# Low-rank decay, learning rate and latent queries from stacked float32r parts instead of float32 matmuls

## The chip, the cores and the metric

The kernel runs on one core of a Trainium2 chip. The metric is the device time of one execution in microseconds (us). Three runs of the kernel before took 1474.29, 1471.72 and 1472.41 us; the median is 1472.41 us. The engines are named as in the profile: PE is TensorE, PEld its weight loads, DVE is VectorE, ACT is ScalarE, POOL is GpSimd, and SP issues DMAs.

## The reference, cut to what matters

Two layers run over 1152 tokens (1024 of a prompt and 8 samples of 16). Each layer projects the normalised input once, and four branches take their columns from it. The change touches two of them: branch A takes two low-rank products of 64 ranks each, and branch B takes its queries from 192 ranks.

```
# branch A: wd and ad are 64 columns each of the shifted projection
w_log = -softplus(-(rw_w0 + tanh(wd) @ rw_w2)) - 0.5
decay = exp(-exp(w_log))
a = sigmoid(rw_a0 + ad @ rw_a2)
kk = normalised(k * rw_kk);  k = k * (1 + (a - 1) * rw_ka)
# per token: s = s * decay + (s @ -kk) (kk * a)^T + v k^T;  y = s @ r
...
# branch B: 192 ranks, 4 heads of 64 + 32 columns
qa = rms_norm(zb[..., :192], mla_qa_g)
q = (qa @ mla_w_uq).reshape(b, t, 4, 96)
q_nope = rms_norm(q[..., :64], ...);  q_rope = rope(rms_norm(q[..., 64:], ...), pos)
# then block-causal attention over keys made from 128 latent ranks
```

Everything is float32.

## The kernel before, in words

Features lie on the 128 partitions and tokens on the columns, in three groups (g = 0, 1, 2) of 384 tokens. Most products go through PE as float32r in three passes: an operand is split in two parts, hi (a float32r copy) and lo (the difference), and hi·hi, hi·lo and lo·hi are summed in PSUM. `project` streams 24 tiles of 128 features per layer in this way (tiles `xh`, `xl`, `wh`, `wl`; 24 matmuls of 384 columns for a tile and group), and small work runs between its matmuls in generators that are advanced by ticks. The order on each engine is that of the program after a scheduler of the tile framework has moved instructions; tiles are rotated through pools of fixed size (`ea` 8, `m` 8, `xl` 3, PSUM `st` 2, `pj` 2, `b` 4).

Stage A opens a layer. The first feature tile WDAD holds the 64 decay ranks on partitions 0 to 63 and the 64 learning-rate ranks on 64 to 127. `shift_sink` mixes each group with its neighbouring token (DVE, L377 to L387) into the tile `z6`, and `tanh_part` (L401 to L405) puts the decay ranks through tanh. `a_elem(i, g, k)` runs six times in a layer, for two halves i of the features and three groups g: `pw` (PSUM `st`) and `pa` (PSUM `b`) are plain float32 matmuls of 64 rows of `wlo` with 64 rows of `z6` (L429 to L432), `pk` is the square sum; then come about a dozen operations on DVE and ACT, among them the running sum (L441) and four products of 64 partitions into `kb` (L471, L477). When all of `kb` and `ar` of a group are there, `systems` builds the chunks' triangular systems with PE, masks them on DVE (`ns`, L504, two buffers) and writes them to DRAM (`nd`). `solve` reads `nd` back, inverts one system per partition in a long alternation of two DVE instructions (L528, L530), and writes the inverses (`dd`, issued by ACT, L542, L543); the recurrence over the chunks starts from these.

Branch B's queries (`query`, L1190 to L1205) come behind the last projection tile. For a head h and a group g, `ps` (PSUM `st`) sums a float32 matmul over ranks 0 to 127 (`qx`, weights behind the keys in `Kt`, an `m` tile) and one over the last 64 ranks (weights `wq1`, which lie in `cx`). ACT squares it (L1196), DVE multiplies it into the tile X (L1198), `split(q, (V, V))` makes hi and lo of the squares on DVE (a cast, L91, and a subtraction, L92), two matmuls sum them over partitions (`b<-sp,cr`), ACT makes the inverse root in two steps (L206, L207), and DVE multiplies (L1205). Eight such units (groups 0 and 1) run in a loop with two ahead, and beside each a `value(j)` (one float32 matmul of 256 columns, one ACT copy, L1211). The four units of group 2 (256 columns) run in a generator beside the prompt attention, which follows. The output projection closes the layer.

Of the kernel before, what the change touches and what calls it, by code (L numbers as in the profile page):

```python
# [10 lines left out]
F32 = mybir.dt.float32  # L11
F32R = mybir.dt.float32r
# [6 lines left out]
D = 1024  # L19
# [11 lines left out]
# projection tiles, in the order in which they are streamed  # L31
# [6 lines left out]
# columns of the per-feature vectors  # L38
# [4 lines left out]
# constant matrices  # L43
# [5 lines left out]
def tile_trunk(ctx: ExitStack, tc: tile.TileContext, *aps):  # L49
# [34 lines left out]
    def split(src, by, view=lambda t: t):  # L84
        """two exact parts of a tile; by: engines of the copy and of the difference"""
# [9 lines left out]
    def total(out, m, parts, start=True, stop=True):  # L95
        """sums over partitions of a tile in two parts, weighted by small integers"""
        mm(out, m, parts[0], start, False)
        mm(out, m, parts[1], False, stop)
# [16 lines left out]
    # Work that runs beside the large products: lanes of generators, each advanced by one step per tick.  # L115
# [37 lines left out]
    # running input of the layer: 4 tiles of [128, 2, G] per token group, and sums of squares  # L153
# [15 lines left out]
    # sums over partitions: of all, of each half; of the halves of queries  # L169
# [21 lines left out]
    def raw_weights(fi, src):  # L191
        """a whole tile of weights ahead of its splitting"""
# [16 lines left out]
    def recip1p(t):  # L209
        """t <- 1 / (1 + t)"""  # L210
# [11 lines left out]
    def load_weights(n):  # L222
        """weights as two exact parts, in pairs of k-tiles in their order of use"""
# [14 lines left out]
    def project(keys, hi, lo, sinks, ticks=(3,)):  # L238
        """one tile of features, or several of them side by side, group after group of tokens"""
# [58 lines left out]
    # zero at the first token of each chunk (64 tokens; 16 in the last 128 columns)  # L298
# [11 lines left out]
    # rows of the chunks' inverses, zero off the diagonal blocks  # L310
    # (half chunks of 64 rows; the room behind each lets the diagonal blocks lie at equal distances)
# [3 lines left out]
    def whole(t, c, cols):  # L315
        """the two halves of chunk c"""
        return t[2 * c:2 * c + 2, 0:128 * cols].rearrange("x (s t) -> x s t", s=64)

    def diagonal(t, i, n, cols, first=0):
        """the n x n blocks of the halves' matrices: block b of rows at columns first + b n"""  # L320
# [14 lines left out]
    for l in range(L):  # L335
        last_layer = l == L - 1
# [968 lines left out]
        for u in units[:2]:  # L1305
            next(u)
# [246 lines left out]
```

## Time and profile before

| | us | share |
|---|---|---|
| median of three runs | 1472.41 | |
| span of the profiled execution (the only time of its own that the page gives) | 1470.1 | |
| PE busy | 1395.4 | 95% |
| DVE busy | 782.2 | 53% |
| ACT busy | 751.9 | 51% |
| POOL busy | 436.8 | 30% |
| TensorE clock, mean granted share | | 0.988 |

The median lies 2.3 us above the span. Busy shares are averages over stages. A float32 matmul stands in the trace as two records ("x2"), a float32r matmul as one. Records of back-to-back matmuls overlap, so that the price of one is read from start to start. The idle time of an engine is put down to the instruction that it then waited for.

### The profile page before, as it was taken

The page shows a single profiled execution, that of the slowest core. Times are in us where ns is not written, and L with a number is a line of the kernel's source. Part 1 is how long each engine was busy: PE and PEld are TensorE (multiplying, and loading weights), DVE is VectorE, ACT ScalarE, POOL GpSimd, SP SyncE. Part 2 cuts the span into 40 slices and gives each one's busy share as a digit, 9 for nine tenths or more (in the row PEclk, how much of TensorE's full clock was granted, in tenths as well). Part 3 has the DMA queues.
Part 4 walks back from the last instruction along what each step waited for, and adds up shares of the span by engine and source line. Part 5 has one row for each costly group of instructions (what it writes and reads, how often), then busy time and mean ns, then how long its engine had stood idle before and what let it go on. Part 6 is the DMA issues. An engine that isn't in the chain of part 4 may idle for free. (4 is left out here: it accounts for less than half of the span.)

```text
span 1470.1 us, 26810 instructions
## 1 busy us (share of the span) xinstructions
PE 1395.4 (95%) x9938; PEld 1158.6 (79%) x9938; DVE 782.2 (53%) x1762; ACT 751.9 (51%) x2017; POOL 436.8 (30%) x575
## 2 busy tenths in 40 slices
PE   4898899999999999999979988999999999999999
PEld 3678778888987776689967787888899778666998
DVE  7985944445136457742387857433632464677211
ACT  6672244655366667642257522455644666666210
POOL 4514314346321110322262333332652111112320
PEclk9999999999999999999989999999999999999999
DMA  7113241111212114033300123221021111131232
GB/s 224 48 33 81 52 101 49 55 46 38 93 42 70 53 31 130 6 114 97 87 22 29 52 66 73 77 69 47 30 78 60 57 53 55 37 109 43 69 96 77
DMA packets 116594, 97.38 MB, mean 66 GB/s; under 512 B 46128, under 2 KB 111344, under 8 KB 116464
## 3 DMA queue, kind: packets, MB, share of 16 engines
q1 hardware_dynamic: 76776, 73.74, 17.1%
q10 hardware_dynamic: 39688, 21.94, 5.0%
q8 instruction: 78, 1.28, 0.4%
q14 instruction: 52, 0.43, 0.1%
HBM read 71.48 MB, written 24.16 MB: 65 GB/s over the span
## 5 line engine op out<-in xcount | busy, mean ns | idle before, releaser
L76 PE MATMUL pj<-xh,wh 128*128 128x384 f32 x1152 | 413.6, 360 | 18.5 <-ACT xh L273 7.3
L76 PE MATMUL pj<-xl,wh 128*128 128x384 f32 x1152 | 395.4, 343 | 4.1 <-POOL xl L275 3.1
L76 PE MATMUL pj<-xh,wl 128*128 128x384 f32 x1152 | 394.8, 343 | 0.0
L235 POOL TENSOR_TENSOR wl<-wr,wh 128x256 fp32r<-128x256 f32 x200 | 155.0, 783 | 484.3 <-ACT wh L234 421.9
L76 PEld LDWEIGHTS pj<-xh,wh 128*128 128x128 f32 x1152 | 220.2, 191 | 45.2 <-ACT sho L390 11.5
L76 PEld LDWEIGHTS pj<-xl,wh 128*128 128x128 f32 x1152 | 220.3, 191 | 11.8 <-POOL xl L275 5.5
L76 PEld LDWEIGHTS pj<-xh,wl 128*128 128x128 f32 x1152 | 220.0, 191 | 7.6 <-issue 6.4
L76 PE MATMUL pj<-yh,wh 128*128 128x384 f32 x384 | 130.0, 339 | 2.4 <-DVE x L1376 2.4
L76 PE MATMUL pj<-yh,wl 128*128 128x384 f32 x384 | 129.2, 336 | 0.0
L76 PE MATMUL pj<-yl,wh 128*128 128x384 f32 x384 | 129.0, 336 | 0.0
L234 ACT ACTIVATE wh<-wr 128x256 fp32r<-128x256 f32 x200 | 80.8, 414 | 93.9 <-PE pj L76 45.9
L76 PEld LDWEIGHTS pj<-yh,wh 128*128 128x128 f32 x384 | 72.5, 189 | 3.7 <-DVE x L1376 2.8
L235 POOL TENSOR_TENSOR wl<-m,wh 128x256 fp32r<-128x256 f32 x56 | 43.5, 787 | 102.2 <-ACT wh L234 75.8
L76 PEld LDWEIGHTS pj<-yh,wl 128*128 128x128 f32 x384 | 72.7, 189 | 0.1
L76 PEld LDWEIGHTS pj<-yl,wh 128*128 128x128 f32 x384 | 72.6, 189 | 0.1
L1251 ACT ACTIVATE X<-b,ng 128x512 f32<-128x512 f32 (+3 forms) x96 | 54.9, 575 | 28.8 <-DVE ng L1243 24.7
L76 PEld LDWEIGHTS st<-X,X 128*64 128x64 f32 x576 | 35.7, 136 | 31.7 <-DVE mx L1239 6.3
L76 PE MATMUL b<-sp,cr 128*128 128x384 f32 (+3 forms) x192 | 58.7, 386 | 1.0 <-POOL sp L92 0.6
L1239 DVE TENSOR_REDUCE mx<-b 128x1 f32<-128x512 f32 (+3 forms) x96 | 53.0, 552 | 8.3 <-PE b L76 6.9
L1372 DVE TENSOR_TENSOR pt<-pj,pt 128x384 f32<-128x384 f32 x24 | 13.4, 557 | 80.6 <-PE pj L76 80.6
L234 ACT ACTIVATE wh<-m 128x256 fp32r<-128x256 f32 x56 | 22.5, 413 | 62.0 <-PE pj L76 60.9
L76 PE MATMUL st<-X,X 128*64 128x128 f32 x576 | 53.6, 283 | 0.3
(295 smaller groups left out, 2556.9 us busy)
## 6 DMA issues: line engine op xcount, KB each, us to landing
wr<-in_win_dram SPq DMA_DIRECT2D x176, 128.0 KB
m<-in_wout_dram SPq DMA_DIRECT2D x12, 512.0 KB
x<-in_xT_dram SPq DMA_DIRECT2D x12, 384.0 KB
ysp<-m ACTq DMA_DIRECT2D x24, 192.0 KB
pt<-in_xT_dram SPq DMA_DIRECT2D x24, 192.0 KB
ea<-ysp SPq DMA_DIRECT2D x24, 192.0 KB
x1d<-x ACTq DMA_DIRECT2D x24, 192.0 KB
pt<-x1d SPq DMA_DIRECT2D x24, 192.0 KB
```

The source lines that it names most:

```text
L76: PE.matmul(out, lhsT=lhsT, rhs=rhs, start=start, stop=stop, skip_group_check=True)
L234: A.activation(out=h, in_=r, func=AF.Copy)
L235: Po.tensor_tensor(out=lo, in0=r, in1=h.bitcast(F32), op=ALU.subtract)
L1239: V.tensor_reduce(out=mx[:, b:b + 1], in_=pc[:, :w], axis=AX.X, op=ALU.max)
L1251: A.activation(out=P[:, :w], in_=pc[:, :w], func=AF.Exp, scale=SCALE, bias=ng, accum_out=sums[pr][:, b, s, h:h + 1])
L1372: V.tensor_tensor(out=xr, in0=ps, in1=xr, op=ALU.add)
```

## The change

Branch A: `wlo` becomes a tile of the `m` pool that holds, for each of the two weights, its hi and lo part with the 64 ranks twice, on both halves of the partitions (eight small DMAs, four ACT copies and four POOL subtractions over the two layers, in place of two DMAs). The shifted WDAD group goes to a passing tile (`gn`), and `tanh_part` writes two `m` tiles `zlr`: for each of decay and learning rate the hi part on one half of the partitions and the lo part on the other. `pw` and `pa` are two float32r matmuls over 128 rows each.

Branch B: the ranks 0 to 127 go in three float32r passes, the last 64 ranks as hi and lo stacked on 128 partitions in two passes; so five float32r matmuls stand where two float32 ones stood. The operands are split once per layer (`query_operand`, `query_weights`) into two tiles of the `xl` pool, `qop` and `qw`. The squares' subtraction goes from DVE to POOL (`split(q, (V, Po))`), and three `value` steps go ahead of the loop. The rest of the diff takes out comments, which shifts line numbers.

```diff
-        wlo = lp.tile([128, 256], F32, tag="wlo", name=nm("wlo"))
-        SY.dma_start(out=wlo, in_=w2a2[l])
+        wlo = mp.tile([128, 2, 2, 256], F32R, tag="m", name=nm("wlo"))
+        for n in range(2):
+            t = s_tile("ea", EA, 256)
+            for half in range(2):
+                SY.dma_start(out=t[64 * half:64 * half + 64], in_=w2a2[l, 64 * n:64 * n + 64])
+            A.activation(out=wlo[:, n, 0], in_=t, func=AF.Copy)
+            Po.tensor_tensor(out=wlo[:, n, 1], in0=t, in1=wlo[:, n, 0].bitcast(F32), op=ALU.subtract)
...
-        z6 = m_tile()
+        zlr = [mp.tile([128, T], F32R, tag="m", name=nm("zlr")) for _ in range(2)]
...
             V.tensor_scalar(out=w, in0=t, scalar1=-2.0, scalar2=1.0, op0=ALU.mult, op1=ALU.add)
+            for n in range(2):
+                z, hi = zs[64 * n:64 * n + 64], zlr[n][64 * n:64 * n + 64, gcols(g)]
+                A.activation(out=hi, in_=z, func=AF.Copy)
+                V.tensor_tensor(out=zlr[n][64 - 64 * n:128 - 64 * n, gcols(g)], in0=z, in1=hi.bitcast(F32),
+                                op=ALU.subtract)
...
-            mm(pw[:, :G], wlo[0:64, i * 128:(i + 1) * 128], z6[0:64, gc])
-            mm(pa[:, :G], wlo[64:128, i * 128:(i + 1) * 128], z6[64:128, gc])
+            for n, p in enumerate((pw, pa)):
+                for part in range(2):
+                    mm(p[:, :G], wlo[:, n, part, i * 128:(i + 1) * 128], zlr[n][:, gc], part == 0, part == 1)
...
-                [shift_sink(WDAD, lambda g: z6[:, gcols(g)], tanh_part),
+                [shift_sink(WDAD, lambda g: s_tile("gn", 3), tanh_part),
...
+        qop, qw = (xp.tile([128, 3072], F32R, tag="xl", name=nm("qop")) for _ in range(2))
...
+        def query_weights(hp_):
+
+            for h in (2 * hp_, 2 * hp_ + 1):
+                cols = slice(128 * h, 128 * h + 128)
+                A.activation(out=w0p[0][:, cols], in_=Kt[h][:, TP:], func=AF.Copy)
+                V.tensor_tensor(out=w0p[1][:, cols], in0=Kt[h][:, TP:], in1=w0p[0][:, cols].bitcast(F32),
+                                op=ALU.subtract)
...
+        def query_operand(g):
...
+            A.activation(out=q1p[0:64, cols], in_=qx[g][0:64, 1, :n], func=AF.Copy)
+            V.tensor_tensor(out=q1p[64:128, cols], in0=qx[g][0:64, 1, :n], in1=q1p[0:64, cols].bitcast(F32),
+                            op=ALU.subtract)
...
-            mm(ps, Kt[h][:, TP:], qx[g][:, 0, :n], True, False)
-            mm(ps, wq1[h], qx[g][0:64, 1, :n], False, True)
+            tok, cols = slice(g * G, g * G + n), slice(128 * h, 128 * h + 128)
+            for i, j in ((0, 0), (0, 1), (1, 0)):
+                mm(ps, w0p[i][:, cols], q0p[j][:, tok], i + j == 0, False)
+            for i in range(2):
+                mm(ps, w1p[i][:, cols], q1p[:, tok], False, i == 1)
...
-            parts = split(q, (V, V))
+            parts = split(q, (V, Po))
...
+        query_operand(0)
+        query_weights(0)
+        for n in range(3):
+            value(n)
+        query_weights(1)
         for u in units[:2]:
             next(u)
+        query_operand(1)
         for n, u in enumerate(units):
             if n + 2 < 8:
                 next(units[n + 2])
-            value(n)
+            if n + 3 < 8:
+                value(n + 3)
             next(u, None)
+        query_operand(2)
```

On DVE in stage A of the second layer, inside `a_elem(0, 1)`, the rows before are (L468, L471, L472 and L474 belong to it; L405 is the tanh of group 2, L377 a shift):

```order
L468 TENSOR_TENSOR ea_8584<-ea_8479,ea_8485 128x384
L405 TENSOR_SCALAR m_8272<-ea_8550 64x384
L471 TENSOR_TENSOR kb_8468<-ea_8470,ea_8584 64x6x64 x2
L472 TENSOR_SCALAR ea_8479<-ea_8479,vcs,nv_8262 128x384
L377 SCALAR_TENSOR_TENSOR m_8280<-pj_8559,vcs,m_8280 128x255
L474 TENSOR_TENSOR ea_8479<-ea_8479,ea_8485 128x384
```

and now (lines shifted by 12: L480, L412, L483 are L468, L405, L471 of before):

```order
L416 TENSOR_TENSOR zlr_8385<-gn_8670,zlr_8385 64x384
L412 TENSOR_SCALAR gn_8670<-ea_8678 64x384
L480 TENSOR_TENSOR ea_8716<-ea_8606,ea_8612 128x384
L483 TENSOR_TENSOR kb_8593<-ea_8595,ea_8716 64x6x64
L416 TENSOR_TENSOR zlr_8384<-gn_8670,zlr_8384 64x384
L483 TENSOR_TENSOR kb_8593<-ea_8595,ea_8716 64x6x64
L484 TENSOR_SCALAR ea_8606<-ea_8606,vcs,nv_8365 128x384
```

The two subtractions of 64x384 for group 2 now stand in the row, one ahead of the tanh and one between the two `kb` products.

On PE in the query loop of the second layer, the rows of one unit before are (`st_14114` is one query, `pj_14124` a value, `b_14127` the sums of the unit two places back):

```order
L76 MATMUL st_14114<-qx_12589,m_12583 128x384
L76 MATMUL st_14114<-qx_12589,cx_12593 128x384
L76 MATMUL pj_14124<-m_12577,cx_12592 128x256
L76 MATMUL b_14127<-sp_14091,cr 128x384
L76 MATMUL b_14127<-sp_14092,cr 128x384
```

and now:

```order
L76 MATMUL st_14342<-qop_14210,qop_14211 128x384 x5
L76 MATMUL pj_14355<-m_12717,cx_12734 128x256
L76 MATMUL b_14358<-sp_14307,cr 128x384
L76 MATMUL b_14358<-sp_14308,cr 128x384
```

The unit keeps its place and its order; only the two float32 matmuls have become five float32r ones (the listing gives both tiles, `qop` and `qw`, the name qop).

On DVE in the same loop the rows before are (L1198 puts a query into X, L91 and L92 are hi and lo of its squares, L1205 ends the unit two places back):

```order
L1198 SCALAR_TENSOR_TENSOR X_14070<-st_14114,vcs,m_12575 128x384
L91 CAST sp_14120<-pt_14117 128x384
L92 TENSOR_TENSOR sp_14121<-pt_14117,sp_14120 128x384
L1205 TENSOR_TENSOR X_14070<-X_14070,pt_14088 128x384
L1198 SCALAR_TENSOR_TENSOR X_14070<-st_14133,vcs,m_12575 128x384
```

and now (L1242 and L1249 are L1198 and L1205 of before):

```order
L1242 SCALAR_TENSOR_TENSOR X_14212<-st_14342,vcs,m_12715 128x384
L91 CAST sp_14351<-pt_14348 128x384
L1249 TENSOR_TENSOR X_14212<-X_14212,pt_14304 128x384
L1242 SCALAR_TENSOR_TENSOR X_14212<-st_14364,vcs,m_12715 128x384
```

The subtraction has left DVE; on POOL the eight subtractions of the loop now stand one behind the other, ahead of all work for the output projection's operands.

## Rows read from the trace of the kernel before

**Rows 1.** Busy time of each engine, from the page (busy us, share of the span, instructions).

```profile
PE 1395.4 (95%) x9938; PEld 1158.6 (79%) x9938; DVE 782.2 (53%) x1762; ACT 751.9 (51%) x2017; POOL 436.8 (30%) x575
```

**Rows 2.** The chain of waits, parts of stage A of the second layer, the first queries and the end (start, us, what).

```profile
838.49 4.54 DMA nd<-ns
...
889.04 0.97 DVE m L530
...
911.44 2.54 ACTq L542
916.14 1.61 PE b L76 x16
...
1260.64 5.04 PE st L76 x12
...
1368.86 97.78 PE pj L76 x564
```

**Rows 3.** Busy time by stretch, stage A (a part of the first layer's and a part of the second's), `solve` and its end in the second, the projection of the last gate (1240 to 1260), the query loop and the start of the attention. Columns: stretch, its length, then busy us (instructions) of PE, PEld, DVE, ACT, POOL, granted clock, DMA share, GB/s.

```profile
20.00:40.00 20.00, 14.86 (x60) 12.70 (x61) 18.57 (x31) 14.76 (x36) 6.82 (x6) 0.91 0.57 125
...
800.00:815.00 15.00, 14.34 (x79) 11.07 (x77) 13.44 (x23) 13.66 (x35) 3.76 (x6) 1.00 0.04 12
866.00:910.00 44.00, 38.23 (x275) 35.85 (x274) 41.25 (x114) 9.22 (x27) 16.68 (x24) 1.00 0.21 56
910.00:917.00 7.00, 4.07 (x29) 3.39 (x29) 0.61 (x2) 1.29 (x5) 0.00 (x0) 0.96 0.82 122
1240.00:1260.00 20.00, 20.00 (x139) 17.33 (x138) 7.15 (x18) 10.69 (x28) 2.86 (x5) 1.00 0.10 34
1260.00:1282.00 22.00, 22.00 (x83) 12.19 (x82) 17.29 (x39) 16.91 (x38) 1.88 (x3) 1.00 0.07 18
1282.00:1300.00 18.00, 17.54 (x95) 10.16 (x94) 14.32 (x49) 12.63 (x40) 0.00 (x0) 1.00 0.41 137
```

**Rows 4.** What DVE waited for from 757 to 866 (line, releaser: us in total, times, longest).

```profile
DVE ns L504 <- DMA nd<-ns: 11.0, 9, 1.6
DVE ea L437 <- PE st L76: 7.0, 3, 2.9
```

**Rows 5.** Groups of instructions by line and shape (count; busy us, mean ns of one; idle before).

```profile
L471 DVE TENSOR_TENSOR kb<-ea,ea 64x384 f32<-64x384 f32 x24 | 17.8, 743 | 0.3
L92 POOL TENSOR_TENSOR sp<-ar,sp 128x384 fp32r<-128x384 f32 x12 | 12.1, 1004 | 25.7 <-ACT sp L89 25.7
L403 ACT ACTIVATE ea<-m 64x384 f32<-64x384 f32 x6 | 3.1, 512 | 0.0
```

**Rows 6.** PE in time at the end of `solve` in the first layer.

```profile
183.40 1.17 PE L76 MATMUL b<-vu,gm 64*64 64x64 f32 x8 [2.92 <-DVE gm L570]
...
185.31 0.52 PE L76 MATMUL pj<-xh,wl 128*128 128x384 f32 x1
185.63 0.52 PE L76 MATMUL pj<-xh,wh 128*128 128x384 f32 x1
```

**Rows 7.** All engines in time, one unit of the query loop in the second layer, and the next one's first matmul.

```profile
1273.89 0.81 PE L76 MATMUL st<-qx,m 128*128 128x384 f32 x2
1274.10 0.58 ACT L206 ACTIVATE pt<-b,eps 128x384 f32<-128x384 f32 x1
1274.17 0.35 DVE L91 CAST sp<-pt 128x384 fp32r<-128x384 f32 x1
1274.62 0.56 DVE L92 TENSOR_TENSOR sp<-pt,sp 128x384 fp32r<-128x384 f32 x1
1274.63 0.91 PE L76 MATMUL st<-qx,cx 64*128 64x384 f32 x2
1274.71 0.52 ACT L207 ACTIVATE pt<-pt 128x384 f32<-128x384 f32 x1
1275.26 0.56 DVE L1205 TENSOR_TENSOR X<-X,pt 128x384 f32<-128x384 f32 x1
1275.47 0.70 PE L76 MATMUL pj<-m,cx 128*128 128x256 f32 x2
1275.58 0.49 ACT L1196 ACTIVATE pt<-st 128x384 f32<-128x384 f32 x1 [0.35 <-PE st L76]
1275.82 0.70 PE L76 MATMUL b<-sp,cr 128*128 128x384 f32 x2
1276.10 0.62 DVE L1198 SCALAR_TENSOR_TENSOR X<-st,vcs,m 128x384 f32<-128x384 f32 x1 [0.28 <-ACT pt L1196]
1276.21 0.38 ACT L1211 ACTIVATE X<-pj 128x256 f32<-128x256 f32 x1
1276.36 0.81 PE L76 MATMUL st<-qx,m 128*128 128x384 f32 x2
```

**Rows 8.** PE in time, a query of group 2 beside the attention.

```profile
1281.13 0.60 PE L76 MATMUL st<-qx,m 128*128 128x256 f32 x2
1281.66 0.70 PE L76 MATMUL st<-qx,cx 64*128 64x256 f32 x2
1282.29 0.49 PE L76 MATMUL b<-m,X 128*128 128x128 f32 x2
```

**Rows 9.** POOL and DVE in time, in the same query loop.

```profile
1268.11 1.01 POOL L1336 TENSOR_TENSOR yl<-ar,yh 128x384 fp32r<-128x384 f32 x1 [6.93 <-ACT yh L1334]
...
1268.48 1.06 DVE L1205 TENSOR_TENSOR X<-X,pt 128x384 f32<-128x384 f32 x1 [0.28 <-ACT pt L207]
```

More of the change, by code (lines that the diff above doesn't have):

```diff
@@ L1183, in tile_trunk @@
         Q2 = []
+        q0p = [qop[:, 1024 * i:1024 * i + 1024] for i in range(2)]
+        q1p = qop[:, 2048:3072]
+        w0p, w1p = ([qw[:, 1024 * j + 512 * i:1024 * j + 512 * i + 512] for i in range(2)] for j in range(2))
+        def query_weights(hp_):
[4 more added lines that the diff above has]
+                                op=ALU.subtract)
+            cols = slice(256 * hp_, 256 * hp_ + 256)
+            w = cx[hp_][0:64, 1, 0:256]
+            for half in range(2):
+                pr = slice(64 * half, 64 * half + 64)
+                A.activation(out=w1p[0][pr, cols], in_=w, func=AF.Copy)
+                V.tensor_tensor(out=w1p[1][pr, cols], in0=w, in1=w1p[0][0:64, cols].bitcast(F32), op=ALU.subtract)
+        def query_operand(g):
+            n = min(G, TP - g * G)
+            cols = slice(g * G, g * G + n)
+            A.activation(out=q0p[0][:, cols], in_=qx[g][:, 0, :n], func=AF.Copy)
+            V.tensor_tensor(out=q0p[1][:, cols], in0=qx[g][:, 0, :n], in1=q0p[0][:, cols].bitcast(F32),
+                            op=ALU.subtract)
+            A.activation(out=q1p[0:64, cols], in_=qx[g][0:64, 1, :n], func=AF.Copy)
+            V.tensor_tensor(out=q1p[64:128, cols], in0=qx[g][0:64, 1, :n], in1=q1p[0:64, cols].bitcast(F32),
+                            op=ALU.subtract)
         def qcols(h, t0, n):
```

## The prediction

> **What bounds the kernel now.** I read the page first: PE is busy for 95% of the span, DVE for 53%, ACT for 51%, POOL for 30% [rows 1]. By that alone each microsecond taken from PE would come off the time. So I read the stages next, with the stretches and the chain of waits. In stage A they tell another story: in 20 to 40 us DVE is busy for 18.57 of 20 and PE for 14.86, in 800 to 815 DVE for 13.44 of 15, and in `solve` DVE for 41.25 of 44 [rows 3]. The chain there runs through writes of `nd`, the two DVE instructions of `solve`, the DMAs of ACT's queue and only then PE [rows 2]. In 910 to 917 PE is busy for 4.07 of 7 [rows 3]: it waits for the recurrence's start. The order places the first products of the recurrence behind the same number of projection matmuls before and after, so what PE saves in stage A it waits longer for at this place. The query loop is the other kind: PE is busy for 22.00 of 22 [rows 3], and the first three queries alone stand in the chain with 5.04 us [rows 2]. The attention behind it has PE at 17.54 of 18, DVE at 14.32 [rows 3]. The end is 97.78 us of projection on PE [rows 2], which the change leaves alone.
>
> **Prices on PE.** 564 float32r matmuls of 384 columns take 97.78 us, 0.173 each [rows 2]. A query unit runs from 1273.89 to 1276.36, that is 2.47 us: 0.74 for the 128-row float32 matmul (to 1274.63), 0.84 for the 64-row one (to 1275.47), 0.35 for the value, 0.54 for the sums [rows 7]. Half the rows do not make a float32 matmul cheaper. Five passes cost 0.87, so a unit needs 0.87 + 0.35 + 0.54 = 1.76 on PE.
>
> **Query loop.** What is late next? ACT has 0.49 + 0.38 + 0.58 + 0.52 = 1.97 a unit, DVE before 0.62 + 0.35 + 0.56 + 0.56 = 2.09 [rows 7]. The subtraction goes to POOL, where its like takes 1.00 [rows 5]; DVE keeps 1.53. But DVE and POOL are not free of each other: the product L1205 took 1.06 in place of 0.56 when it fell beside a POOL subtraction from 1268.11 to 1269.12 [rows 9, 7]. If cast and product may not run beside the subtraction, one unit takes at least 0.35 + 0.56 + 1.00 = 1.91 of the two engines, with L1198 beside it (it reads PSUM and one tile). That is under ACT's 1.97, if the product comes ahead of the subtraction. It can: it belongs to the unit two places back, stands right behind the cast on DVE, and ACT has ended its root long before. I take 2.1 a unit, ACT's 1.97 and some of the 0.28 to 0.35 that handovers cost in these rows. Eight units give 8 x (2.47 - 2.1) = 3.0; the last unit's subtraction takes 1.00 and not 0.56, so 2.5 us a layer are left, 5.0 in both. Bounds: none (the cycle stays at 2.47), and 8 x (2.47 - 1.97) = 4.0 a layer.
>
> **The lock by the skill.** The row above shows one delayed product [rows 9]. The Trainium skill (SBUF — State Buffer, "Who interferes with whom") says that a DVE instruction with two SBUF inputs, or a copy or cast in a two-port mode, and a GpSimd instruction that reads SBUF hold a shared port for the whole instruction, and that issue order decides who blocks. The trace agrees on the product: 1.06 for 0.56. By that rule a subtraction that gets in right behind the cast would hold the product back by its whole length, and then the next L1198 too; that is the second rival below.
>
> **Queries of group 2.** Before, one takes 0.53 + 0.63 = 1.16 (1281.13 to 1282.29) [rows 8]; five passes of 256 columns by 0.173 x 256/384 are 0.58. Four of them save 2.3 us a layer on PE. PE is all but full there, though DVE is not far behind, so some of it becomes waiting: I take 1.8 a layer, 3.6 in all, between 0.5 and 2.3 a layer.
>
> **Operands of the queries.** 14 ACT copies and 14 DVE subtractions a layer are new, some 4 to 5 us on each (a 64x384 copy takes 0.51 [rows 5], a 128x384 subtraction 0.56 [rows 7]). The scheduler has put them beside the last gate's projection, where DVE is busy for 7.15 and ACT for 10.69 of 20 us [rows 3]. They are hidden as long as the two tiles come free in time; they take `xl` buffers that groups 0 and 1 of that same projection free. If the last weights come late the first query does: I count +0.5 for both layers, between 0 and 2.
>
> **Stage A.** Removed: 12 float32 matmuls a layer of 0.84, added 24 of 0.173, 5.9 us of PE a layer, which count at nothing where PE waits anyway. Added: six DVE subtractions of 64x384 and six ACT copies of 0.51 a layer. The nearest row for the subtraction is the `kb` product of the same shape, 0.74 in the mean of 24 with collisions [rows 5], about 0.55 without. So 3.3 to 4.5 us of DVE a layer. In the second layer DVE has waited 7.0 us in three places for PE's `st` [rows 4]; the first group's pair, and some of the second's, fall into these waits, and each `pw` or `pa` is 0.84 - 0.35 = 0.49 shorter: with two of them ahead of the second wait and four ahead of the third these end up to 1 and 2 us sooner. The last group's pair, 1.1 to 1.5 us, meets a DVE that is busy for 13.44 of 15 [rows 3]. I take +1.0 there, between -1 and +3.5. In the first layer DVE has no such slack (18.57 of 20), so nearly all of 3.3 counts, less 1.3 for two to three products that end 0.49 sooner each: +2.0, between 0 and +4.5. What is late there is late for `nd`, `solve`, `dd` and the recurrence, the whole chain [rows 2]. The copies and subtractions of `wlo` and their small DMAs lie beside the preparation of the inputs and count at nothing; without that cover the first `pw` would wait for one more POOL subtraction, 1.00 x 256/384 = 0.7 us.
>
> **The sum.** +1.0 + 2.0 (stage A) - 5.0 (query loops) - 3.6 (group 2) + 0.5 (operands) = -5.1 us. Against the span of 1470.1 that is 1465.0; the median of the runs lies 2.3 higher, at 1472.41, so I forecast 1467.3. With all terms at their good ends the time would be 1472.4 - 1 - 8 - 4.6 = 1458.8, with all at their bad ends 1472.4 + 8 + 0 - 1 + 2 = 1481.4.
>
> **Rivals.**
> - PE sets everything, as the 95% suggest. Then all that PE saves counts: 2 x 5.9 in stage A and 2 x (8 x 0.71 + 2.3) in the queries, 27.8 us, or 1444.6. Against it: the idle PE of stage A [rows 3] and the chain there [rows 2]. Chance 0.04.
> - The subtraction on POOL gives the query loop's gain back. If it starts before the product, a unit takes 0.62 + 0.35 + 1.00 + 0.56 = 2.5, as long as before. Then +3.0 - 3.6 + 0.5 = -0.1: 1472.3. For it speak the delayed product [rows 9] and that POOL has no other work in the loop; against it that DVE's next instruction stands ready when the cast ends, while POOL has yet to be told. Chance 0.24.
> - Slower: stage A's subtractions all come late on the chain. It decides once a layer's stage A grows by more than (5.0 + 3.6 - 0.5)/2 = 4.1 us over before. Six subtractions at 0.74, and the waits for their ACT copies (0.51 each, behind other work on ACT, 13.66 of 15 busy [rows 3]) at three of six, make 6.0 a layer; PE, which then waits longer than the 2.92 us of before, drops to the lower clock (0.32 a matmul in place of 0.173 behind that wait [rows 6]) for some more of its work. 12.0 - 8.1 = +3.9: 1476.3. For it: in 20 to 40 DVE is nearly full. Against it: the 7.0 us of waits in the second layer. Chance 0.20.
> - The forecast itself: 0.52.
>
> **How the numbers follow.** What a measurement of this kernel can tell from no change is 0.2%, 2.9 us: the lines are 1469.5 and 1475.3. The forecast's own range is 1462 to 1471, so of its 0.52 about 0.46 are faster and 0.06 are the same. With the first rival, and a little of the second (0.04), faster has 0.54. The second rival's other 0.18, the forecast's 0.06 and a little of the third (0.03) make 0.27 the same; 0.17 and the second's last 0.02 make 0.19 slower. The range must take in the second rival and most of the third: 1460 to 1477.
>
> **What the profile after would show.** Right: `st` matmuls from `qop` at 0.173 from start to start, units of the query loop at 2.0 to 2.2 us with PE no longer gapless there; the recurrence's first `b` matmul 0 to 2 us later relative to the layer's start; DVE's waits for `st` in the second layer's stage A shorter than 7.0 in total. Wrong: units at 2.5 us with L1249 at over 1 us (second rival), a start of the recurrence more than 4 us later in each layer (third), or earlier than before, which would mean that the shorter PE products and not DVE set stage A.

## The result, and the profile after

The changed kernel takes 1482.32 us (median of six runs, 1477.42 to 1485.83) against 1473.29 us of the kernel before beside it (six runs, 1471.72 to 1475.24). The ratio is 1.0057, 95% interval 1.0035 to 1.0078: slower, by 9.0 us in the medians. The forecast was 1467.3 with a range up to 1477. The profiled execution has a span of 1482.7 us and a mean granted clock of 0.976, where before had 1470.1 and 0.988. Of all runs in this document one is left out of its median: a run of `b_hold`, below, took 7239.62 us at a full clock, nearly five times as long as the ten others of that kernel.

Engines of the changed kernel, from the page, as in [rows 1]:

```profile
PE 1384.2 (93%) x9962; PEld 1178.4 (79%) x9962; DVE 796.1 (54%) x1778; ACT 764.4 (52%) x2061; POOL 470.7 (32%) x603
```

PE is busy for 11.2 us less and the span is 12.6 us longer: there is a saving on PE, and the time in which PE waits has grown by more. To see where, I followed one chain of landmarks through both traces. The first is the recurrence's first matmul, after in both layers and then before in the second ([rows 6] has before's first layer, at 183.40):

```profile
195.53 0.29 PE L76 MATMUL b<-vu,gm 64*64 64x64 f32 x2 [2.76 <-DVE gm L582]
923.24 1.18 PE L76 MATMUL b<-vu,gm 64*64 64x64 f32 x8 [2.72 <-DVE gm L582]
```

```profile
907.27 0.29 PE L76 MATMUL b<-vu,gm 64*64 64x64 f32 x2 [2.76 <-DVE gm L570]
```

The wait in front of it is as long as before (2.72 to 2.92), and it comes later. With the start of the second layer (748.99 before, 758.11 after), the start of the queries, the first query of group 2 and the output projection read from PE in time in the same way, each stage has its own difference:

| stage | before | after | difference |
|---|---|---|---|
| first layer: start to recurrence | 183.40 | 195.53 | +12.13 |
| recurrence to first query, first layer | 353.80 | 355.57 | +1.77 |
| second layer: start to recurrence | 158.28 | 165.13 | +6.85 |
| recurrence to first query, second layer | 353.30 | 353.20 | -0.10 |
| query loop, to group 2's first query, second layer | 20.56 | 14.60 | -5.96 |
| from there to the output projection, second layer | 83.71 | 86.55 | +2.84 |
| query loop, first layer | 20.89 | 14.62 | -6.27 |
| from there to the output projection, first layer | 83.65 | 85.13 | +1.48 |

The projections behind the two attentions differ by 0.10 or less. So the query side gained, and stage A lost 19 us in the two layers together. A stage's figure is that of one execution: in the runs below that leave stage A as it was (`q_only`, `q_vv`), it came out at 184.22 and 185.19 in the first layer and 160.81 and 159.16 in the second, so that about 2 us of any one of these says nothing.

The whole of the second layer's stage A, from its start to the recurrence, before and after (columns as in [rows 3]):

```profile
748.99:907.27 158.28, 140.68 (x861) 120.69 (x861) 122.77 (x261) 74.45 (x189) 58.94 (x76) 0.97 0.17 46
758.11:923.24 165.13, 139.94 (x862) 126.86 (x861) 127.53 (x268) 78.03 (x197) 62.47 (x78) 0.93 0.17 44
```

PE's busy time hardly fell here (139.94 for 140.68), though its cheaper matmuls should have saved 5.9 us: at a granted clock of 0.93 in place of 0.97 more of its matmuls took 0.32 us, as behind the wait in [rows 6], and not 0.173. DVE is busy for 4.8 us more, and it waits no less than before: 37.6 us in place of 35.5.

Busy time by stretch, the changed kernel's own stage A (20 to 40, and 809 to 824, which lies 9 us after the 800 to 815 of before, as its layer starts 9 us later) and the query loop; columns as in [rows 3]:

```profile
20.00:40.00 20.00, 12.87 (x48) 10.38 (x47) 14.84 (x25) 10.64 (x25) 3.88 (x4) 0.89 0.55 113
809.00:824.00 15.00, 12.28 (x56) 11.27 (x55) 11.21 (x23) 10.49 (x25) 1.32 (x4) 0.77 0.06 17
...
1276.00:1291.00 15.00, 13.94 (x74) 12.33 (x71) 13.03 (x26) 13.49 (x33) 9.43 (x8) 1.00 0.15 46
```

In the first two, PE, DVE and ACT are all busy for less of the time than in [rows 3] (DVE 14.84 for 18.57, ACT 10.49 for 13.66): three engines that wait for each other. In the second the granted clock is 0.77, between the two levels of 1.2 and 2.4 GHz, where it was 1.00, behind a PE that had idled (for 0.75, 0.76 and 2.72 us between 803 and 812). One such wait can be read directly, ACT and SP in time at the start:

```profile
34.03 0.52 ACT L273 ACTIVATE xh<-ea 128x384 fp32r<-128x384 f32 x1 [0.74 <-DVE ea L271]
34.69 4.16 SPq L368 DMA_DIRECT2D ea<-in_w2a_dram  x4
...
40.14 0.42 ACT L369 ACTIVATE wlo<-ea 128x256 fp32r<-128x256 f32 x1 [5.58 <-DMA ea<-in_w2a_dram]
40.49 0.52 ACT L273 ACTIVATE xh<-ea 128x384 fp32r<-128x384 f32 x1
```

The copy of `wlo` stands on ACT between two copies of `xh` and waits 5.58 us for the small loads, which SP issues from 34.69 on. The next copy of `xh`, for which PE waits, stands behind it. And these are the split low-rank values, all 12 of each in the two layers:

```profile
L416 DVE TENSOR_TENSOR zlr<-gn,zlr 64x384 fp32r<-64x384 f32 x12 | 9.6, 799 | 1.9 <-ACT zlr L415 1.6
L415 ACT ACTIVATE zlr<-gn 64x384 fp32r<-64x384 f32 x12 | 6.2, 516 | 0.3 <-DVE gn L412 0.2
```

The query loop, all engines in time, one unit, as in [rows 7]:

```profile
1282.83 1.03 PE L76 MATMUL st<-qop,qop 128*128 128x384 f32 x5
...
1283.56 0.65 DVE L91 CAST sp<-pt 128x384 fp32r<-128x384 f32 x1
...
1283.70 0.59 PE L76 MATMUL pj<-m,cx 128*128 128x256 f32 x2
1283.94 0.70 PE L76 MATMUL b<-sp,cr 128*128 128x384 f32 x2
1284.24 0.56 DVE L1249 TENSOR_TENSOR X<-X,pt 128x384 f32<-128x384 f32 x1
1284.36 1.31 POOL L92 TENSOR_TENSOR sp<-pt,sp 128x384 fp32r<-128x384 f32 x1 [0.36 <-DVE sp L91]
...
1284.48 1.03 PE L76 MATMUL st<-qop,qop 128*128 128x384 f32 x5
```

A unit takes 1.65 us, from 1282.83 to 1284.48, where it took 2.47. PE has no gap in it: 0.87 for the five matmuls of the query, 0.24 for the value, 0.54 for the sums. The cast takes 0.65 beside the subtraction of the unit before, 0.35 in [rows 7]; the product stands ahead of the subtraction and is not delayed, and the subtraction takes 1.31.

### The profile page after: what moved, and what is told of

The parts are those of the page before. It is cut to its first block, busy times and chain, and to the rows that moved or that the text cites. A ratio compares the mean times of both kernels' runs of the same rounds, so it can differ in the third digit from the quotient of the medians.

```text
span 1482.7 us, 26999 instructions
## 1 busy us (share of the span) xinstructions
PE 1384.2 (93%) x9962; PEld 1178.4 (79%) x9962; DVE 796.1 (54%) x1778; ACT 764.4 (52%) x2061; POOL 470.7 (32%) x603
## 5 line engine op out<-in xcount | busy, mean ns | idle before, releaser
L76 PE MATMUL pj<-xh,wh 128*128 128x384 f32 x1152 | 418.2, 363 | 38.1 <-ACT sho L396 12.7
L76 PE MATMUL pj<-xl,wh 128*128 128x384 f32 x1152 | 401.0, 348 | 3.8 <-POOL xl L275 3.4
L76 PE MATMUL pj<-xh,wl 128*128 128x384 f32 x1152 | 398.8, 346 | 0.0
L76 PEld LDWEIGHTS pj<-xh,wh 128*128 128x128 f32 x1152 | 223.7, 194 | 61.5 <-ACT sho L396 17.5
L76 PEld LDWEIGHTS pj<-xl,wh 128*128 128x128 f32 x1152 | 224.4, 195 | 11.1 <-POOL xl L275 5.9
L76 PEld LDWEIGHTS pj<-xh,wl 128*128 128x128 f32 x1152 | 223.6, 194 | 5.0 <-issue 3.8
L1306 PE MATMUL pj<-cm,X 128*128 128x128 f32 x288 | 48.3, 287 | 5.0 <-ACT X L1295 5.0
```

The source lines that it names most:

```text
L76: PE.matmul(out, lhsT=lhsT, rhs=rhs, start=start, stop=stop, skip_group_check=True)
L1306: PE.transpose(ptp[:, j * 128:(j + 1) * 128], Pb[slot][:, j * 128:(j + 1) * 128], ident)
```

## The experiments

Five sets of runs; a difference is that of a kernel's median to the median of before in its own set (1472.21, 1472.69, 1473.05, 1472.65 and 1473.10).

**Which half loses.** Stage A and the queries were each changed alone. `q_only` is the changed kernel with stage A's five edits taken back, `a_only` the kernel before with these five edits, and `q_vv` is `q_only` with one more word changed:

```diff
-            parts = split(q, (V, Po))
+            parts = split(q, (V, V))
```

> Queries as changed, stage A as before. By the landmarks of the two traces the queries gain 4.3 us in the first layer and 2.9 in the second, and stage A loses 12.1 and 6.9. If the two parts are independent, this kernel is 7 us faster than before: about 1466. If the query part itself disturbs the next stages (operands of the output projection, the m and xl pools), it is 0 to 3 us faster only.

> As q_only, but the subtraction of the squares stays on DVE. If DVE and POOL exclude each other as my second rival has it, DVE alone (2.09 us a unit) is about as fast as the pair: within 1 us of q_only. If POOL is a real relief, a unit goes from about 2.0 to 2.1 or 2.2 and the kernel is 1 to 3 us slower than q_only.

> Stage A as changed, queries as before. If the loss is stage A's alone: 1473 + 19 = about 1490 where the profiled run of after is met, 1484 to 1492 with its spread from run to run. If stage A loses only together with the queries (through pools or the order): about 1473.

Measured: `q_only` 1466.05 (ratio 0.9955, 0.9944 to 0.9967), -6.2 us; `q_vv` 1462.02 (0.9928, 0.9916 to 0.9939), -10.2; `a_only` 1487.61 (1.0106, 1.0093 to 1.012), +15.4. -6.2 and +15.4 give the +9.0 of the whole change within 0.2: nothing shows that the two halves touch each other. In the trace of `a_only` the two stages A are 18.8 us longer than before (196.06 and 164.38); 4.0 of it is gone again by the end, in stages that no edit touched and whose figures move by that much between other runs too. The subtraction on POOL costs 4.0 us. `q_vv` is the fastest version of this study.

**One fault at a time in stage A.** Five edits, each against one suspect. `early_wlo`: the changed kernel, where `wlo` of the first layer is loaded and split at the start of the program. The others are edits of `a_only`. `a_late`: raw weights in a tile of their own, split behind the first tanh (`if g == 0: split_wlo()`). `a_nosub`: no subtraction of the values (the lower parts are zeros that POOL sets once a layer, so those product terms are missing). `a_poolsub`: the same subtraction on POOL (`Po` for `V`). `a_warm`: the clock, by six matmuls more ahead of each `pw`, whose sums are overwritten.

```diff
+            for _ in range(6):
+                mm(pw[:, :G], ONES, xh[g][:, 0, :])
             for n, p in enumerate((pw, pa)):
```

> The change with one edit: the low-rank weights of the first layer are loaded and split at the start of the program. In the trace of after ACT stands 5.6 us at the first of these copies, for their DMAs, and xh, DVE and PE wait behind it (5.4 and 4.1 us). Theory that this stall makes nearly half of the first layer's loss: the recurrence of the first layer starts 4 to 6 us earlier than in after, and the time falls by that, to about 1477. Theory that DVE's six added subtractions set the stage: they are as many as before, and the time changes by less than 1 us.

> a_only with one edit: the low-rank weights are still loaded at the layer's start, but into an m tile, and their ACT copies and POOL subtractions are issued with the tanh of the first token group and no longer ahead of it, so that ACT does not stand at them before the copies of the normalised input (the early load had only moved the delay: it put the first input 6.6 us later). Stall theory: the first layer's recurrence starts 4 to 5.5 us earlier than a_only's 196.1, the second layer's stage keeps its length; 1487.6 becomes 1482 to 1484. Theory that the subtractions on DVE set the stage and the stall lies in their shadow: less than 1.5 us earlier.

> a_only without DVE's six subtractions a layer; the lo halves of the decay and learning-rate operands are zeros, written once a layer by POOL (this leaves out the lo part of those operands). DVE theory: 0.55 to 1.25 us each and what they wait for, 3 to 5 us a layer: 1487.6 becomes 1478 to 1481. Stall and clock theories: the copies on ACT, the stall and the waits of PE remain, and less than 2 us a layer comes back: 1484 to 1487.

> a_only with the six subtractions of a layer on POOL in place of DVE. If DVE's own time is what counts: 2 to 4 us a layer come back, 1480 to 1484. If DVE and POOL exclude each other, as L1205 in the query loop showed, the same time is lost in another place and pw waits longer for a slower subtraction: 1487 to 1492.

> a_only with six more float32r matmuls ahead of each pw, written over by pw itself, so that PE works where it waited for zlr. They add 36 x 0.173 = 6.2 us of PE work a layer at the higher clock. Clock theory (PE's waits bring the lower clock, at which projection matmuls take 0.32 and stage A becomes bound by PE): the time at the lower clock falls from some 60 us towards 35, and the kernel is 2 to 5 us faster than a_only in spite of the added work. Theory that PE is what stage A waits for: 4 to 12 us slower. Neither: within 2 us.

Measured: `early_wlo` 1482.80 (1.0070, 1.0052 to 1.0087), as the changed kernel; `a_late` 1487.83 (1.0103), `a_nosub` 1487.23 (1.0094), `a_warm` 1487.63 (1.0107, 1.0090 to 1.0124), all as `a_only`; `a_poolsub` 1490.63 (1.0118, 1.0103 to 1.0133), 2.5 more over before than `a_only`, by intervals that overlap. None of the five gave time back, so each theory that had promised a gain missed. In two of them the traces show why. PE in `early_wlo` up to 60 us, then in `a_nosub` in time:

```profile
PE st L76 <- DVE ea L163: 23.2, 3, 18.7
```

```profile
43.43 1.01 PE L76 MATMUL b<-zlr,wlo 128*128 128x384 f32 x2 [8.11 <-POOL zlr L405]
```

In `early_wlo` PE waits 18.7 us in one piece for the first sum of squares, where it waited 10.1 in the changed kernel: the loads came ahead of the input's, and what the copies no longer waited was lost at the start. In `a_nosub` the zeros were set on POOL behind the subtraction of `wlo`, and PE waited 8.11 for them. A zero in place of a subtraction is no free edit when it is written by an engine that stands still. In `a_late` ACT no longer waited for the loads and the first layer's recurrence started 3.0 us earlier (193.06), but the time is that of `a_only`; PE waited 3.8 us for a subtraction instead. The clock is another matter, from the view by core of `a_only` and of `a_warm`:

```profile
core 0: 1484.8 us, clock 0.979
```

```profile
core 0: 1482.3 us, clock 0.986
```

This execution of `a_warm` was the fastest of its four. The clocks of all four are 0.986, 0.982, 0.981 and 0.979, those of `a_only` 0.980, 0.979, 0.979 and 0.975. So filling PE brought back little of the clock and none of the time, and the added matmuls take time of their own: the run doesn't tell what the clock costs. Time and clock do go together: the six runs of the changed kernel stand in the order of their clocks, from 1477.42 us at 0.984 to 1485.83 at 0.970. Whether the lower clock makes a run longer, or longer waits of PE lower the clock, no run here separates.

**The order.** The listing of ACT's program gave a theory: in the changed kernel the first K0 sink (the copy that empties K0's first PSUM tile) stands in row 64 of ACT's program and not in row 47, because tiles of one tag get their buffers in the order of their first writes, and `wlo` and `zlr` are written ahead of K0's. In the program PE then has its 24 matmuls of WDAD's group 1 almost in a block, and they no longer alternate with K0's. `a_mend2` is `a_only` with the order mended: the tanh is called behind K0's sink, `wlo` is loaded and split there, and the sink has a higher priority.

```diff
-                [shift_sink(WDAD, lambda g: s_tile("gn", 3), tanh_part),
-                 shift_sink(K0, lambda g: zk0[:, gcols(g)], lambda g, zs: start("a", a_elem(0, g, zs)))])
+                [shift_sink(WDAD, lambda g: s_tile("gn", 3), wdad.__setitem__),
+                 shift_sink(K0, lambda g: zk0[:, gcols(g)], lambda g, zs: (tanh_part(g, wdad.pop(g)), start("a", a_elem(0, g, zs))))])
```

`b_hold` is the converse: the kernel before, with its K0 sink made late and nothing else (the sink goes to row 61). `mended_vv` is the mended order in the whole change, with the subtraction of `q_vv`.

```diff
         z6 = m_tile()
+        hold = [m_tile(1) for _ in range(2)]
...
+            if g == 0:
+                for t in hold:
+                    V.tensor_copy(out=t[0:64], in_=w[:, 0:1])
```

> Stage A changed as in a_only (same matmuls, same copies and subtractions of wlo and zlr, queries as before), but so written that the first K0 sink comes before the tanh in ACT's program, as it does in the kernel before, and PE's program alternates the inputs of WDAD and K0 of group 1 again. Theory A (the loss is the order: a late K0 sink keeps a PSUM buffer, PE can't alternate, idles, and its clock falls): the first recurrence matmul of layer 0 comes near 184 to 188 us instead of 196, time 1470 to 1479 us. Rival B (the loss is the added work itself, copies, subtractions, DMAs, the K=128 matmuls, wherever they stand): still 1484 to 1490 us.

> The kernel before with no matmul, split or load changed: two more tiles of the tag m are taken ahead of zk0, and two copies of one column (64x1) behind the tanh of group 0 write them first, so that zk0 gets its slot, and the first K0 sink its place on ACT, only behind the tanh. Theory A: the order alone makes the loss: time 1479 to 1488 us, first recurrence matmul of layer 0 at 190 us or later, more time at the low clock than the 36.8 us of before. Rival B (the added work makes the loss): 1472 to 1474.5 us, as before.

> The changed kernel with stage A in the mended order of a_mend2 and the query subtractions all on DVE as in q_vv. Theory A: 1461 to 1470 us; below q_vv's 1462.0 only if the fewer passes in stage A are worth more than their copies and subtractions. Rival B: 1474 to 1481 us (q_vv plus the loss of a_only).

Measured: `a_mend2` 1481.42 (1.006, 1.0046 to 1.0073), +8.4; `b_hold` 1473.72 without the one long run (1474.17 with it; 1.0001, 0.9992 to 1.001), +0.7; `mended_vv` 1471.02 (0.999, 0.9981 to 0.9999), -2.0. The late sink alone costs nothing that can be told from noise, so the theory fell. What `a_mend2` gained lies in the first layer (its recurrence starts at 188.15 in place of 196.06) and nothing in the second (165.82 from the layer's start, `a_only` 164.38). In the first layer it also took away ACT's wait for the loads, so that its 7.0 us can't be put down to the order.

**The added work alone.** The last question was whether the added instructions cost by themselves or because matmuls wait for them. A first pair, `b_sub` and `b_both`, put the 12 copies and 12 subtractions into the kernel before, with the old matmuls, without and with the late sink; nobody reads the result. `a_mend2_nosub` is `a_mend2` without the subtractions.

> The kernel before, all matmuls, loads and the query parts as they were, with the 12 copies (ACT, 64x384) and 12 subtractions (DVE, 64x384) of the split low-rank values added in the two layers' stage A; nobody reads what they make. The K0 sink stays early on ACT. Theory C (the added split work, put in the middle of ACT's and DVE's programs at the time when DVE sets the pace, is what costs): 1477 to 1483 us. Rival D (the split work alone lies beside other work; the cost comes from the matmuls' new dependence on it): 1472 to 1475 us.

> b_hold (late first K0 sink) and b_sub (split work that nobody reads) together in the kernel before, its matmuls as they were. If late sink and split work add up and are together the cause: 1479 to 1488 us. If what the pieces do depends on the matmuls that wait for the splits (rival D): 1472 to 1477 us, near b_hold's 1474.2.

> a_mend2 without its 12 DVE subtractions (the lower parts of the low-rank values are left at zero, set once a layer on POOL, so that product terms of the third kind are missing); copies, matmuls, weights' parts and the mended order stay. Theory C with the subtractions as the price: 1473 to 1478 us, the first recurrence matmul of layer 0 at or before 186 us. If copies, loads and matmul operands are the price and not the subtractions: 1480 to 1483 us, as a_mend2 (1481.4).

Measured: `b_sub` 1484.75 (1.0084, 1.007 to 1.0097), +12.1; `b_both` 1483.66 (1.0068, 1.0054 to 1.0083), +11.0; `a_mend2_nosub` 1479.63 (1.0049, 1.0037 to 1.0062), 1.4 less over before than `a_mend2`, by intervals that overlap. In its trace the second layer's stage A is 3.2 us shorter than that of `a_mend2` (162.65 from the layer's start) and the first layer's 1.9 longer. The work alone costs as much as the whole change does, or more; the late sink adds nothing to it. But `b_sub`'s result takes a tile of the tag `ea` for each group, which moves other instructions. So the last set writes the change's own tiles in the change's own order. `b_zlr`:

```diff
         z6 = m_tile()
+        zlr = [mp.tile([128, T], F32R, tag="m", name=nm("zlr")) for _ in range(2)]
...
             V.tensor_scalar(out=w, in0=t, scalar1=-2.0, scalar2=1.0, op0=ALU.mult, op1=ALU.add)
+            for n in range(2):
+                z, hi = zs[64 * n:64 * n + 64], zlr[n][64 * n:64 * n + 64, gcols(g)]
+                A.activation(out=hi, in_=z, func=AF.Copy)
+                V.tensor_tensor(out=zlr[n][64 - 64 * n:128 - 64 * n, gcols(g)], in0=z, in1=hi.bitcast(F32),
+                                op=ALU.subtract)
```

`b_zlr_copy` has the copies only, `b_zlr_sub` the subtractions only (`in1=z`). `b_all` is `b_zlr` with the change's loads, copies and subtractions of the weights besides; its ACT program is that of `a_only` but for a few rows, and its matmuls are the old ones. In all four the first K0 sink is late, as in `b_hold`, which priced that at +0.7.

> The kernel before with everything that the change adds in stage A (the weights' loads, copies and subtractions, the values' copies and subtractions, in tiles of the tag m, in the order of a_only on ACT), but with the old matmuls of 64 rows; nobody reads the parts. Theory C (the added work makes the loss, the matmuls' new form gains little): 1484 to 1492 us, layer 0 late by about 12 us at its first recurrence matmul, layer 1 by about 7. Rival D (the matmuls' wait for the parts makes the loss): 1472 to 1480 us.

> b_all without the weights' part: only the copies and subtractions of the values. Theory C: each layer's stage A late by about 7 us, 1480 to 1486 us; what b_all has beyond it (about 5 us, in layer 0) is the weights' loads on SP and ACT's wait for them. Rival D: 1472 to 1476 us.

> b_zlr with the 12 ACT copies alone. If the copies carry the loss (ACT's program is held at each copy until DVE has made the tanh, and sinks stand behind it): 1479 to 1485 us. If the subtractions carry it: 1473 to 1477 us.

> b_zlr with the 12 DVE subtractions alone (each takes a value from itself, so that no copy is needed). If DVE's time carries the loss: 1478 to 1484 us. If the copies carry it: 1473 to 1476 us; my term in the prediction (3 us in all) would give 1476.

| kernel | us | over before | ratio, 95% |
|---|---|---|---|
| `b_zlr_copy` | 1478.45 | +5.4 | 1.0041, 1.0026 to 1.0057 |
| `b_zlr_sub` | 1479.97 | +6.9 | 1.0049, 1.0036 to 1.0062 |
| `b_zlr` | 1484.49 | +11.4 | 1.0080, 1.0066 to 1.0093 |
| `b_all` | 1490.97 | +17.9 | 1.0132, 1.0112 to 1.0152 |

This shows what the loss comes from. Copies and subtractions add up (5.4 + 6.9 = 12.3, together 11.4), and with the weights' part (6.5 more) the old kernel has lost as much as `a_only`'s 15.4, or more, without one matmul changed. By which way they cost is seen only in places. One for a copy stands in `b_zlr_copy`, ACT and DVE in time in the second layer, and then in what DVE waits for there from 749 to 850:

```profile
785.23 0.51 ACT L211 ACTIVATE ea<-ea 64x384 f32<-64x384 f32 x1
785.76 0.52 ACT L409 ACTIVATE zlr<-m 64x384 fp32r<-64x384 f32 x1
786.31 0.94 ACT L212 ACTIVATE ea<-ea 64x384 f32<-64x384 f32 x2
786.86 0.35 DVE L406 TENSOR_SCALAR m<-ea 64x384 f32<-64x384 f32 x1 [1.36 <-ACT ea L212]
```

```profile
DVE m L406 <- ACT ea L212: 2.7, 2, 1.4
```

The copy stands on ACT between the two steps of a tanh, DVE waits 1.36 for the second step, and everything of that group behind it; in the trace of before the same step (L405) has no idle time ahead of it in that stretch:

```profile
L405 DVE TENSOR_SCALAR m<-ea 64x384 f32<-64x384 f32 x3 | 1.8, 610 | 0.0
```

But before, too, DVE waited there for the same line of ACT, at two other instructions:

```profile
DVE ea L468 <- ACT ea L212: 1.5, 2, 0.8
DVE ea L441 <- ACT ea L212: 1.2, 2, 0.6
```

In `b_zlr_copy` these are 0.2 and 0.7, and its wait for PE's `st` is 4.8 where [rows 4] has 7.0. So this wait shows one way in which a copy delays DVE; that it makes up the 5.4 is not shown.

How a subtraction costs, in `b_zlr`, DVE in time:

```profile
802.65 0.97 DVE L477 TENSOR_TENSOR kb<-ea,ea 64x384 f32<-64x384 f32 x1
803.63 1.00 DVE L410 TENSOR_TENSOR zlr<-m,zlr 64x384 fp32r<-64x384 f32 x1
804.64 1.00 DVE L477 TENSOR_TENSOR kb<-ea,ea 64x384 f32<-64x384 f32 x1
```

It stands between the two halves of a `kb` product, on an engine without a gap, so its 1.00 us is added to the path of this `kb` in full. The groups of the runs with one kind alone:

```profile
L409 ACT ACTIVATE zlr<-m 64x384 fp32r<-64x384 f32 x12 | 6.2, 517 | 2.2 <-DVE m L406 2.1
```

```profile
L409 DVE TENSOR_TENSOR zlr<-m 64x384 fp32r<-64x384 f32 x12 | 7.8, 647 | 0.3
```

6.2 us of copies cost 5.4, 7.8 us of subtractions cost 6.9. By the medians a microsecond put on either engine here cost some nine tenths of a microsecond of the whole; by the intervals 3.8 to 8.4 us for the copies and 5.3 to 9.1 for the subtractions.

Three things stay open. `b_all` loses 17.9 and `a_only` 15.4, so the shorter matmuls seem to gain some 2.5 us, but the two intervals overlap; and in `b_all` the old weights' load stands behind the four new ones and PE waited 5.7 us for it, so the 6.5 of the weights' part and this gain may both be smaller. And `a_nosub` had no gain in the second layer either (164.53 from the layer's start, `a_only` 164.38), though subtractions cost 6.9 with the old matmuls; PE waited only 0.6 for the zeros there, so they don't explain it. And how much of the loss goes by way of TensorE's clock is not known: the median run of `b_zlr`, with the old matmuls, has the same mean clock as that of `a_only`, 0.979.

## Why the prediction was wrong

**The step that failed is the sum for stage A**: +1.0 in the second layer and +2.0 in the first, against +15.4 for both in `a_only`. It failed in three terms.

- *The copies of the values counted at nothing.* The term named them (six a layer, 0.51 each) and went on with DVE alone, as though ACT had room. [rows 3] had ACT at 13.66 of 15 there. They cost +5.4 (`b_zlr_copy`).
- *The subtractions got credits.* 3.3 to 4.5 us a layer were near the truth: 7.8 us in both without the copies, 9.6 in the changed kernel. But I set 1 to 2 us of earlier `st` products and 7.0 us of DVE's waits against them. DVE's wait for `st` did get shorter, as forecast, 5.9 for the 7.0 of [rows 4] (766 to 880 in the changed kernel):

```profile
DVE ns L516 <- DMA nd<-ns: 11.7, 10, 2.0
DVE ea L449 <- PE st L76: 5.9, 3, 2.6
...
DVE gn L412 <- ACT ea L212: 1.9, 2, 1.1
```

  but over the whole stage DVE's waits grew, from 35.5 to 37.6 us, with 1.9 for the tanh on ACT among them. The subtractions alone cost +6.9 (`b_zlr_sub`), nearly their whole length.
- *The weights' parts counted at nothing*, beside "the preparation of the inputs", with 0.7 us if that cover was gone. The preparation of the inputs was the path: ACT makes `xh`, and held 5.58 us in the midst of it. They cost up to 6.5 (`b_all` less `b_zlr`).

The matmuls, which would have to pay for this, gain some 2.5 by the medians, not clear of noise. I had that right (they "count at nothing where PE waits anyway").

**The third rival** had the direction and the place: 6.0 us a layer, and its sign, a start of the recurrence over 4 us late in each, came (12.13 and 6.85). Its 12.0 stands for a measured 15.4; its mechanism, subtractions and the waits for their copies, is what `b_zlr` shows with 11.4, and the loads in the first layer are what it lacked. I gave it 0.20 because of the waits for `st`, a slack that belongs to DVE and not to the chain that DVE and ACT form together. Its clock part is neither shown nor excluded: the clock fell as it said, and `a_warm` did not separate it.

**The queries** were forecast at -5.0 - 3.6 + 0.5 = -8.1 and measured at -6.2 (`q_only`), but that came near by luck, by two errors against each other. In the traces the loop is 12.2 us shorter (5.96 + 6.27), where I had 5.0, and what follows is 4.3 longer, where I had a gain of 3.6. A part of both is work that changed places: the last unit's sums (0.54) and six small matmuls of the attention (0.69) now stand behind group 2's first query, and one value (0.35) ahead of the first query. PE in time, before (that query starts at 1281.13, [rows 8]) and after (it starts at 1291.04):

```profile
1280.44 0.85 PE L76 MATMUL b<-m,X 128*128 128x128 f32 x6
```

```profile
1291.63 0.33 PE L76 MATMUL b<-sp,cr 128*128 128x384 f32 x1
1291.80 0.61 PE L76 MATMUL b<-m,X 128*128 128x128 f32 x4
1292.16 0.42 PE L76 MATMUL b<-sp,cr 128*128 128x384 f32 x1
```

Without it the loops gained some 9 us and group 2 lost some 2: PE's waits there rose from 1.1 to 3.5 us in the second layer, so that what its matmuls saved came out as waiting. The loops gained more than I had because a unit takes 1.65 and not 2.1. The bound of 1.97 from ACT was no bound: I summed ACT's records, which overlap as PE's do. In the unit from 1282.83 ACT is busy for 1.62 by the view of stretches, and PE and DVE for as much:

```profile
1282.83:1284.48 1.65, 1.65 (x11) 1.60 (x10) 1.62 (x4) 1.62 (x5) 1.28 (x2) 1.00 0.00 0
```

PE fills the unit without a gap; my 1.76 for it had the value at 0.35, which takes 0.24 here. Three engines are full to within 0.03 us, so no one of them can be called the limit. Two ACT records of 0.51 stand in the rows of `b_zlr_copy` above as one of 0.94, an overlap of 0.08. The Trainium skill (ScalarE: Activation LUTs, "What ACT_TABLE_LOAD costs") says that back-to-back ACTIVATEs overlap by some 93 ns; the trace agrees with 0.08. The operands are hidden as far as the traces can tell: from the recurrence to the first query the layers took 1.77 more and 0.10 less, and kernels with the old queries differ by more than that there (352.48 to 355.75 in the first layer). Of the three values that the code puts ahead of the loop, only one stands there on PE.

**The second rival** is right in part. The unit is not back at 2.5, but `q_vv` shows that the subtraction on POOL gives 4.0 us of the gain back. In the trace of `q_vv` the cast takes its 0.35 again, a unit takes 1.68, nearly the same, and the loop is 12.98 long for 14.60. What is saved there is the wait for the last subtraction, which the changed kernel has ahead of group 2's first query (PE in time), and 0.54 of sums that stand behind that query in `q_vv`:

```profile
1290.75 0.45 PE L76 MATMUL b<-sp,cr 128*128 128x384 f32 x1 [0.93 <-POOL sp L92]
1291.04 0.75 PE L76 MATMUL st<-qop,qop 128*128 128x256 f32 x5
```

From the first query to the output projection both layers together take 200.6 us in `q_only` and 197.2 in `q_vv`, so 3.4 of the 4.0 lie in that stretch. For the lock I had feared that the product would be held. Here it was the cast of the next unit, at 0.65 for 0.35, and the subtraction itself, at 1.31 for 1.00. The Trainium skill's rule (SBUF — State Buffer, "Who interferes with whom") names casts as well as products and lets the order of issue decide; the trace agrees, for the product began 0.12 us ahead of the subtraction (1284.24 and 1284.36) and kept its 0.56.

**The first rival** is excluded: PE is busy for 11.2 us less, and the kernel is not faster but slower.

## What to carry to other kernels

Splitting an operand to make a matmul cheaper moves work from PE to the engines that feed it. Before counting its gain, look whether PE waits in that very stage; if DVE and ACT pass a value back and forth there, price each added copy and subtraction at nearly its full length, whatever the page's average says of the engine. Price a copy of weights by the instruction that stands behind it in the same queue, and test added work by itself: put it into the old kernel with nobody reading it.

## What was not expected of the hardware and the order

Taking one wait away gave nothing alone (the loads' wait in `early_wlo` and `a_late`), since another wait ended just behind; only adding pieces to the kernel before gave a sum, 5.4 + 6.9 against 11.4. The late sink of `b_hold` moved 14 rows of ACT's program and stopped PE's alternation, and cost 0.7 us, inside the interval of no change. In the query loop PE, DVE and ACT came out full at the same time, 1.62 to 1.65 us of a unit of 1.65.
